# Another share of the gathers into the second stage's own tile, and fewer planned gather steps in the third

## Chip, core and metric

One core of one Trainium2 chip runs the whole layer as one program. The metric is device time in microseconds (us), the median of the runs shown. Times inside the program are read from the trace of one profiled execution and count from the start of its span.

## What is computed

One decoder layer on 256 tokens of width 2048: a mixer of two head groups, then PEER, a product-key retrieval over 128 x 128 single-neuron experts. Nearly all that follows is PEER:

```
s_half = einsum('thpd,hpkd->thpk', q, sub_keys);  v_half, i_half = top_k(s_half, 16)
top_s, pick = top_k(cand_s, 16)               # 8 heads x 16 = 128 experts per token
gates = softmax(top_s)
a    = einsum('cd,ced->ce', hc, w_u[ec])      # each token against its 128 rows of u
coef = gates * gelu(a)
out  = einsum('ce,ced->cd', coef, w_v[ec])    # weighted sum of its 128 rows of v
```

then a gated residual add and a last RMSNorm. u and v are 16384 x 2048 each.

## The kernel before

Most tokens go the dense way: every row of u and v is streamed and multiplied on TensorE (PE), and the gates are put in as a one-hot matrix. The last 64 tokens (and, for the first half of the experts, a few more) go the sparse way: for one expert slot per step, an indirect DMA gathers 128 rows of u or v (1 MB) into a tile of 128 x 2048, here called a room, and VectorE (DVE) takes one pass over it.

PEER runs in four stages of 64 blocks. In the text they are **u0, v0, u1, v1**: the u products of the first half of the experts, the v products of that half, and the same for the second half.

- A **u block** (u_block, L815 as the recording helper's line) loads 1 MB of u and makes 32 matmul passes of 128 x 144 (psU). Between blocks PE makes the gate matrix of a group of 8 tokens (pg) from one-hot tiles o and eq that DVE builds. ACT applies the gelu (tile ge), DVE multiplies it in (X).
- A **v block** (v_group, matmuls at L1088) loads 1 MB of v into a tile named raw, splits it on ACT (whi, L1062) and DVE (wlo, L1065), and makes 20 matmuls of 128 x 512 into eight accumulators (acc). wlo has two buffers, so DVE can be at most two blocks ahead of PE. At the end of v0 the eight accumulators are copied into the tile s2 (COPY s<-acc), half by ACT and half by DVE. At the end of v1 they are folded (pc, with the sparse sum sp) into the output.

**The sparse steps.** `steps_` walks a fixed plan: 32 steps m, 6 u, 16 o, 58 u, 64 v. A u, m or o step is one SCALAR_TENSOR_TENSOR on DVE with an accumulated dot product (L939); a v step adds a weighted row tile to sp (L945, first one L943). `sparse` does a step where the tables STEPS and a counter say so; `fetch` issues gathers ahead, at most `most[0]` of them. The last o step is followed by a gelu of its dot products on ACT (o_gelu, shown as ACTIVATE doto), which is put in program order among ACT's casts.

**The rooms.** `gather` takes a room: `flip` counts modulo `turns[0]`. Where it is not zero and one of the two halves of `spare[0]` is free, that half is taken; otherwise `other[0]()` gives a tile. In v0 the spare is s2 and the other one is more_room, whose tag `more` has two buffers; until the o steps are over, one of these holds h2m, the vector that they multiply with. From block 48 of v0 on, three rooms without s2 are used (rows3 is the third).

**What sets the order.** A scheduler that simulates the program chooses the order of the instructions of each engine; the order is then fixed, and on the chip each engine takes its instructions in turn. Gathers (on POOL), the sparse steps (on DVE) and what is marked with `pin` keep the order of the program among themselves, and the rest is put between them. Gathers and the DMAs that accumulate are issued by POOL (queue q0), the streams of u and v by SP (queue q1). One of POOL's is at block 20 of u1 in the code: `s<-s` adds the second half of a 64-token part of s2 onto the first by an accumulating DMA, and `s<-x2d` later refills what it read.

Of the kernel before, what the change touches and what calls it, by code (L numbers as in the profile page):

```python
# [32 lines left out]
HALF = 64  # L33
# [8 lines left out]
NS = S - TD  # L42

STEPS = dict(u0=[j for j in range(6, HALF - 6) if j % 8 != 1], v0=[j for j in range(HALF - 2) if j % 6 != 5],
             u1=[j for j in range(HALF - 6) if j % 6 != 1])


NM = 32
# [73 lines left out]
def body(ctx, tc, a, out, dbg=None, stop=None):  # L122
# [53 lines left out]
    x2 = xT.rearrange("p k s -> p (k s)").rearrange("p (t d) -> p t d", t=2)  # L176
# [38 lines left out]
    def row_load(dst, row, n=1):  # L215

        nc.gpsimd.dma_start(dst, bass.AP(tensor=row.tensor, offset=row.offset, ap=[[P // 16 * D, n], [0, P // n], [1, D]]))
# [531 lines left out]
    with ExitStack() as gctx:  # L749
# [73 lines left out]
        spare, free, other = [None], [0, 1], [None, None]  # L823
        most = [3]
        flip, turns = [0], [3]
# [164 lines left out]
        def last_room(pool):  # L990
            turn3[0] += 1
            return more_room() if turn3[0] % 3 else pool.tile([P, D], F32, name="rows3")
# [3 lines left out]
            return late.tile([P, D], F32, name="rows", tag="more", bufs=2)  # L996

        def v_group(hf, s2, late, fin=None):
            spare[0], other[0], most[0], turns[0] = x2 if hf else s2, more_room, 3, 2
            if hf:  # L1000
                fetch()
            with tc.tile_pool(name=f"vsb{hf}", bufs=1) as vb:
# [16 lines left out]
                for j in range(HALF):  # L1019
# [1 line left out]
                    tick()  # L1021
                    fixed[0] = False
                    if hf == 1:
                        if j == 0:
                            turns[0] = 3
                        elif j == 30:
                            g2 = fin("g2")
                            row_load(g2, row5, 16)
                        elif j == 34:
                            pin(nc.vector.tensor_mul(s2[:, 0, :], s2[:, 0, :], g2))  # L1030
                            nc.gpsimd.dma_start(s2[:, 0, :], x2d[:, 0, :], accum_op=OP.add)
                        elif j == 36:
                            pin(nc.vector.tensor_mul(s2[0:NS, 1, :], s2[0:NS, 1, :], g2[0:NS, :]))
                            nc.gpsimd.dma_start(s2[NS:P, 1, :], x2d[NS:P, 1, :])
                            nc.gpsimd.dma_start(s2[0:NS, 1, :], x2d[0:NS, 1, :], accum_op=OP.add)
                        elif j == 45:
                            other[0], most[0] = None, 2
                        elif j == 47:
                            gf = fin("gf")
                            nc.gpsimd.dma_start(gf, a["gfin"])  # L1040
                    elif j == 48:
                        spare[0], other[0], most[0] = None, lambda: last_room(vb), 3
                    elif j == 57:
                        other[0], most[0] = more_room, 2
# [478 lines left out]
        s2 = late.tile([P, 2, D], F32, name="s2")  # L1523
# [3 lines left out]
        dump("idx", idx)  # L1527
        uctx.close()
        v_group(0, s2, late)
        with tc.tile_pool(name="oh1", bufs=1) as oh[0]:  # L1530
            u_half(up, 1, s2)
        fixed[0] = False
        v_group(1, s2, late, lambda n: late.tile([P, D], F32, name=n, tag="more", bufs=2))


# [20 lines left out]
```

## Time and profile before

| | us |
|---|---|
| median of 3 runs | 1887.3 (1884.8 to 1891.29) |
| the profiled execution | 1885.83 |
| its span | 1883.8 |
| PE busy | 1783.8 (95%) |
| DVE busy | 1519.9 (81%) |
| POOL busy | 396.9 (21%) |

So 2.0 us of the profiled execution lie outside the span, and it stands 1.5 us below the median. PE's busy share says little by itself, since it is an average over stages and a matmul that waits inside a busy stretch is not seen in it; the chain of waits and the timelines of single engines are read instead. In a timeline a row has its start, its length, the engine, the line, the tiles, a count, and in brackets the idle time before it and who ended that. A step of 2.29 us starts 2.21 us after the one ahead of it where nothing is waited for, because reading and writing overlap at the seam. A POOL row is the time to issue a DMA, not the time in which it moves data.

### The profile page before, as it was taken

How to read it: one execution, taken by the hardware profiler on the slowest of the kernel's cores; microseconds unless marked ns; L12 is line 12 of the kernel's file. 1: busy time of each engine (PE TensorE's matmuls, PEld its weight loads, DVE VectorE, ACT ScalarE, POOL GpSimd, SP SyncE). 2: the span in 40 equal slices, each digit the busy share in tenths (PEclk: the TensorE clock that was granted, in tenths of full speed). 3: DMA queues.
4: the chain of work that ended last, by engine and by line, in shares of the span. 5: the costliest groups of instructions: out<-in, count | busy, mean ns of one | idle time of the engine just before them, and what ended most of it. 6: DMA issues, size and time to landing. Idle time of an engine off the chain costs nothing.

```text
span 1883.8 us, 29116 instructions
## 1 busy us (share of the span) xinstructions
PE 1783.8 (95%) x11560; PEld 1567.1 (83%) x11560; DVE 1519.9 (81%) x2354; ACT 707.8 (38%) x1278; POOL 396.9 (21%) x289
## 2 busy tenths in 40 slices
PE   5899999999879999999999699999999999999997
PEld 3899888798669999999997477778889898777774
DVE  7988889899689997599867799986657737889876
ACT  3444454645344421111144255541111114454554
POOL 1000001011010022111111434433112112444520
PEclk9999899999999999999999899999999999999999
DMA  8989888889888679999989899999999998999992
GB/s 343 396 324 371 300 301 301 345 302 336 306 295 322 249 262 357 425 426 424 424 347 353 314 424 425 425 379 323 426 426 426 426 418 356 407 370 360 413 357 98
DMA packets 97434, 672.51 MB, mean 357 GB/s; under 512 B 11905, under 2 KB 12177, under 8 KB 19025
## 3 DMA queue, kind: packets, MB, share of 16 engines
q1 hardware_dynamic: 66818, 467.78, 63.8%
q0 software_dynamic: 30480, 202.88, 27.0%
q8 instruction: 91, 1.49, 0.3%
q14 instruction: 45, 0.37, 0.1%
HBM read 662.81 MB, written 5.41 MB: 355 GB/s over the span
## 4 chain that ended last, share of the span: by engine, by line
PE 69%; DMA 15%; issue 7%; DVE 5%; POOL 2%; ACT 1%; SPq 0%; POOLq 0%; ACTq 0%; DVEq 0%
PE acc L1088 25%; PE psU L815 16%; PE psN L455 9%; DMA raw<-in_u 7%; PE psA L245 5%; PE psD L356 3%; PE bkB L356 2%; DMA s<-in_urow,sm__5028 2%; DVE raw L204 2%; DMA raw<-in_adaT 1%; DMA s<-in_urow,sx 1%; PE bkC L356 1%; DVE wlo L164 1%; PE bvB L408 1%; PE pg L815 1%
## 5 line engine op out<-in xcount | busy, mean ns | idle before, releaser
L815 PE MATMUL psU<-xT,raw 128*128 128x160 f32 (+1 forms) x4096 | 550.0, 295 | 16.4 <-DMA raw<-in_u 14.3
L815 PEld LDWEIGHTS psU<-xT,raw 128*128 128x128 f32 x4096 | 535.3, 191 | 21.0 <-ACT ge L815 14.2
L1088 PE MATMUL acc<-whi,cc 128*128 128x512 f32 x1512 | 371.7, 393 | 15.7 <-ACT whi L1062 15.7
L1088 PEld LDWEIGHTS acc<-whi,cc 128*128 128x128 f32 x1512 | 284.8, 189 | 86.6 <-ACT whi L1062 16.1
L1065 DVE TENSOR_TENSOR wlo<-raw,whi 128x2048 fp32r<-128x2048 f32 x126 | 288.4, 2289 | 78.9 <-issue 46.5
L1062 ACT CAST whi<-raw 128x2048 fp32r<-128x2048 f32 x126 | 240.7, 1911 | 41.8 <-DMA raw<-in_v 41.6
L1088 PE MATMUL acc<-wlo,cc 128*128 128x512 f32 x1008 | 254.9, 392 | 1.1 <-DVE wlo L1065 0.9
L204 DVE SCALAR_TENSOR_TENSOR raw<-raw,crow 128x2048 f32<-128x2048 f32 x96 | 219.3, 2285 | 22.5 <-DMA raw<-in_adaT 22.3
L163 ACT CAST whi<-raw 128x1024 fp32r<-128x1024 f32 (+1 forms) x174 | 168.6, 1019 | 165.0 <-DMA raw<-in_winA 33.1
L164 DVE TENSOR_TENSOR wlo<-raw,whi 128x1024 fp32r<-128x1024 f32 (+1 forms) x174 | 201.1, 1182 | 27.5 <-ACT whi L163 25.1
L1088 PEld LDWEIGHTS acc<-wlo,cc 128*128 128x128 f32 x1008 | 161.9, 161 | 63.7 <-DVE wlo L1065 3.3
L455 PE MATMUL psN<-whi,act 128*128 128x512 f32 x512 | 167.1, 402 | 1.4 <-ACT act L679 0.7
L815 ACT ACTIVATE X<-psU 128x160 f32<-128x160 f32 (+18 forms) x91 | 23.7, 260 | 289.1 <-PE psU L815 289.1
L455 PEld LDWEIGHTS psN<-whi,act 128*128 128x128 f32 x512 | 96.2, 190 | 25.6 <-issue 1.7
L455 PE MATMUL psN<-wlo,act 128*128 128x512 f32 x256 | 104.0, 406 | 5.7 <-DVE wlo L164 5.7
L831 POOL DMA_INDIRECT xT<-in_v,sx x25 | 79.1, 3165 | 121.9 <-DVE sp L945 79.4
L831 POOL DMA_INDIRECT rows<-in_urow,sx x35 | 69.5, 1985 | 143.6 <-DVE rows L939 109.7
L1051 ACT CAST cc<-X 128x192 fp32r<-128x192 f32 x126 | 44.0, 353 | 145.7 <-PE acc L1088 145.4
L939 DVE SCALAR_TENSOR_TENSOR rows<-rows,h2t 128x2048 f32<-128x2048 f32 x35 | 79.7, 2287 | 19.9 <-DMA rows<-in_urow,sx 19.9
L245 PE MATMUL psA<-act,whi 128*128 128x256 f32 x480 | 88.1, 286 | 3.9 <-ACT whi L163 3.9
L815 DVE TENSOR_TENSOR X<-X,ge 128x144 f32<-128x144 f32 (+17 forms) x92 | 24.2, 269 | 76.3 <-ACT ge L815 75.9
L831 POOL DMA_INDIRECT rows<-in_v,sx x28 | 51.8, 1848 | 136.5 <-DVE X L815 61.7
(376 smaller groups left out, 2595.6 us busy)
## 6 DMA issues: line engine op xcount, KB each, us to landing
raw<-in_u SPq DMA_DIRECT2D x128, 1024.0 KB, 20.6
raw<-in_v SPq DMA_DIRECT2D x128, 1024.0 KB, 11.3
raw<-in_adaT SPq DMA_DIRECT2D x96, 1024.0 KB, 7.1
raw<-in_winN SPq DMA_DIRECT2D x16, 1024.0 KB, 7.0
raw<-in_woutN SPq DMA_DIRECT2D x16, 1024.0 KB, 6.9
raw<-in_wqT SPq DMA_DIRECT2D x16, 1024.0 KB, 5.7
raw<-in_winB SPq DMA_DIRECT2D x16, 832.0 KB, 6.4
raw<-in_winD SPq DMA_DIRECT2D x12, 1024.0 KB, 6.5
```

Of the source, the lines that this page charges most:

```text
L163: nc.scalar.copy(hi[:, sl], r[:, sl])
L164: nc.vector.tensor_sub(lo[:, sl], r[:, sl], hi[:, sl].bitcast(F32))
L204: nc.vector.scalar_tensor_tensor(r, r, 1.0, crow, op0=OP.mult, op1=OP.mult, accum_out=modc[:, j, k:k + 1])
L245: nc.tensor.matmul(p_, x[:, sl], y[:, k, :], start=k == 0 and n == 0, stop=k == KB - 1 and n == 2)
L356: nc.tensor.matmul(bank[:, b, :], x[:, w], y[:, k, :], start=k == k0 and n == 0 and first, stop=k == k1 - 1 and n == 2, skip_group_check=True)
L455: nc.tensor.matmul(ps[tt], x[:, k, ts_], y[:, w], start=k == 0 and j == 0, stop=k == KB - 1 and j == 2)
L815: i = f(*a, **k)
L831: pin(nc.gpsimd.indirect_dma_start(out=r, out_offset=None, in_=src, in_offset=bass.IndirectOffsetOnAxis(ap=o, axis=0)))
L939: pin(nc.vector.scalar_tensor_tensor(r, r, 1.0, h, op0=OP.mult, op1=OP.mult, accum_out=d[:, e:e + 1]))
L1062: inorder(nc.scalar.copy(hi, r))
L1065: nc.vector.tensor_sub(lo[:, i:i + n], r[:, i:i + n], hi[:, i:i + n].bitcast(F32))
L1088: return nc.tensor.matmul(acc[c][0:m], x, w[:, c[1] * 512:(c[1] + 1) * 512], start=jj == 0 and n == 0, stop=jj == HALF - 1 and n == 2 - c[ ...
```

## The change

Two numbers. In v_group, turns starts at 3 in place of 2, in both halves (in v1 it became 3 at block 0 before): of three gathers two are sent to the halves of s2 in v0, where it was every second one. In u1 the table STEPS names three blocks in four for a sparse step, where it was five in six.

```
-             u1=[j for j in range(HALF - 6) if j % 6 != 1])
+             u1=[j for j in range(HALF - 6) if j % 4 != 1])
...
         def v_group(hf, s2, late, fin=None):
-            spare[0], other[0], most[0], turns[0] = x2 if hf else s2, more_room, 3, 2
+            spare[0], other[0], most[0], turns[0] = x2 if hf else s2, more_room, 3, 3
...
                     if hf == 1:
-                        if j == 0:
-                            turns[0] = 3
-                        elif j == 30:
+                        if j == 30:
```

The sparse steps of the three stages stay the same in number and in kind. Counted over DVE's rows between the stages' first and last passes, v0 has 52 of them before and 43 in the change, u1 44 and 51, v1 38 and 40. Three places are shown.

DVE in v0 from the pass wlo of block 15, before. A row with rows or s_6398 and h2m is an o step; s_6398 is s2.

```order
L1065 TENSOR_TENSOR wlo<-raw,whi 128x2048
L1052 TENSOR_TENSOR cc<-X_6392,cc 128x192
L939 SCALAR_TENSOR_TENSOR rows,doto<-rows,h2m 128x2048
L1065 TENSOR_TENSOR wlo<-raw,whi 128x2048
L939 SCALAR_TENSOR_TENSOR s_6398,doto<-s_6398,h2m 128x2048
L939 SCALAR_TENSOR_TENSOR rows,doto<-rows,h2m 128x2048
L939 SCALAR_TENSOR_TENSOR s_6398,doto<-s_6398,h2m 128x2048
L939 SCALAR_TENSOR_TENSOR rows,doto<-rows,h2m 128x2048
L1052 TENSOR_TENSOR cc<-X_6392,cc 128x192
L939 SCALAR_TENSOR_TENSOR s_6398,dots<-s_6398,h2t 128x2048
```

Behind the pass of block 16 stand four o steps in a row, two of them in rooms of the tag `more`.

The same place in the change, DVE again, from the pass of block 14.

```order
L1063 TENSOR_TENSOR wlo<-raw,whi 128x2048
L1050 TENSOR_TENSOR cc<-X_6392,cc 128x192
L1063 TENSOR_TENSOR wlo<-raw,whi 128x2048
L1050 TENSOR_TENSOR cc<-X_6392,cc 128x192
L1063 TENSOR_TENSOR wlo<-raw,whi 128x2048
L939 SCALAR_TENSOR_TENSOR s_6398,doto<-s_6398,h2m 128x2048 x2
L939 SCALAR_TENSOR_TENSOR rows,doto<-rows,h2m 128x2048
L1050 TENSOR_TENSOR cc<-X_6392,cc 128x192
L1063 TENSOR_TENSOR wlo<-raw,whi 128x2048
```

Three o steps stand there, one in each of three rooms, and the last one before them is three blocks up. On ACT the gelu of doto stands behind the cast of block 16 in both.

DVE at the end of v0 and the start of u1, before: from the two o tiles of the first group on. eq, iota, idx, gat belong to the one-hot tiles.

```order
L815 TENSOR_TENSOR o_11049<-eq,gat 128x512 x2
L1065 TENSOR_TENSOR wlo<-raw,whi 128x2048
L1052 TENSOR_TENSOR cc<-X_7357,cc 128x192
L815 TENSOR_TENSOR eq<-iota_5020,idx 128x512
L1065 TENSOR_TENSOR wlo<-raw,whi 128x2048
L815 TENSOR_TENSOR o_11076<-eq,gat 128x512 x2
L939 SCALAR_TENSOR_TENSOR rows,dots<-rows,h2t 128x2048 x2
L1142 COPY s_6398<-acc_8935 128x512
```

The one-hot tiles of the first two groups are made ahead of the copies. Three more copies follow.

The same place in the change, from the last copy on.

```order
L1140 COPY s_6398<-acc_8941 128x512
L939 SCALAR_TENSOR_TENSOR rows_10530,dots<-rows_10530,h2t 128x2048
L939 SCALAR_TENSOR_TENSOR rows,dots<-rows,h2t 128x2048 x2
L939 SCALAR_TENSOR_TENSOR rows_10629,dots<-rows_10629,h2t 128x2048
L939 SCALAR_TENSOR_TENSOR rows,dots<-rows,h2t 128x2048 x2
L939 SCALAR_TENSOR_TENSOR rows_10758,dots<-rows_10758,h2t 128x2048
L815 TENSOR_TENSOR o_11040<-iota_5020,idx 128x1024
L815 TENSOR_TENSOR eq<-iota_5020,idx 128x512
L815 TENSOR_TENSOR o_11067<-iota_5020,idx 128x1024
L939 SCALAR_TENSOR_TENSOR rows,dots<-rows,h2t 128x2048
L815 TENSOR_TENSOR o_11042<-eq,gat 128x512 x2
```

Eight steps of the plan that stood among v0's blocks now stand between the copies and the second one-hot tile of the first group, o_11042. On PE three u blocks stand ahead of the first pg in both. On POOL `s<-s` now stands behind the gather of the third of these eight, and `s<-x2d` behind that of the fifth; before, they stood behind the twelfth and the fifteenth gather counted from the same one.

DVE at the end of v1, before.

```order
L945 SCALAR_TENSOR_TENSOR sp<-xT,dots,sp 128x2048
L1065 TENSOR_TENSOR pair_15282<-raw,pair_15282 128x1024 x2
L1065 TENSOR_TENSOR pair_15288<-raw,pair_15288 128x1024 x2
L945 SCALAR_TENSOR_TENSOR sp<-xT,dots,sp 128x2048
L1104 TENSOR_TENSOR tg<-pc,g_14288 128x512
```

One step (xT is the spare tile of v1, with two halves) stands behind the last passes of v.

The same in the change.

```order
L945 SCALAR_TENSOR_TENSOR sp<-xT,dots,sp 128x2048
L1063 TENSOR_TENSOR pair_15272<-raw,pair_15272 128x1024 x2
L1063 TENSOR_TENSOR pair_15278<-raw,pair_15278 128x1024 x2
L945 SCALAR_TENSOR_TENSOR sp<-xT,dots,sp 128x2048 x4
L1102 TENSOR_TENSOR tg<-pc,g_14274 128x512
```

Four steps stand there, in two rooms; before each of the last two its gather has to wait for the step two ahead of it.

## The prediction

> **What bounds the kernel now.** I read the chain of waits first, then the stages by windows, then PE's timeline where the chain leaves PE.
>
> ```profile
> 1094.92 185.14 PE acc L1088 x809
> 1281.22 12.04 PE psU L815 x96
> 1293.27 25.64 DMA raw<-in_u
> ...
> 1330.49 33.44 DMA raw<-in_u
> 1368.25 34.90 DMA raw<-in_u
> ...
> 1471.23 34.84 DMA raw<-in_u
> ...
> 1571.32 272.20 PE acc L1088 x1192
> 1849.01 4.63 DVE pair L1065 x4
> 1853.64 2.27 DVE sp L945
> ```
>
> v0 and v1 are PE: 809 matmuls in 185.14 us, so a block of 20 takes 4.577 us. u1 is partly the stream of u: four stretches of it are waits for DMA. The very end goes over DVE, its last sparse step included.
>
> ```profile
> 971.00:1281.00 310.00, 292.96 (x1269) 224.74 (x1267) 270.57 (x242) 146.04 (x188) 114.42 (x49) 0.97 0.95 384
> 1281.00:1571.00 290.00, 273.86 (x2479) 269.23 (x2480) 172.82 (x251) 45.40 (x170) 56.07 (x50) 0.99 0.99 402
> 1571.00:1884.00 313.00, 300.20 (x1299) 229.36 (x1297) 260.10 (x201) 155.36 (x212) 111.93 (x41) 0.99 0.88 341
> ```
>
> The rows are v0, u1, v1; behind PE, PEld, DVE, ACT and POOL stand the granted clock, the DMA share and GB/s. In u1 the queues are full (0.99), in v1 not (0.88). v0 has 17 us in which PE does nothing, though no engine is full. The change touches nothing ahead of v0. Four places decide; I sum them against the profiled execution, 1885.83.
>
> **A, the stall in the middle of v0: removed, -17.5.**
>
> ```profile
> 1044.94 1.09 PE L1088 MATMUL acc<-whi,cc 128*128 128x512 f32 x4
> 1061.73 3.75 PE L1088 MATMUL acc<-whi,cc 128*128 128x512 f32 x8 [15.70 <-ACT whi L1062]
> ...
> 1059.43 0.21 ACT L815 ACTIVATE doto<-doto 128x16 f32<-128x16 f32 x1 [24.69 <-DVE rows L939]
> 1059.55 0.33 ACT L1051 CAST cc<-X 128x192 fp32r<-128x192 f32 x1
> 1059.79 1.89 ACT L1062 CAST whi<-raw 128x2048 fp32r<-128x2048 f32 x1
> ...
> 1038.39 2.28 DVE L939 SCALAR_TENSOR_TENSOR s<-s,h2m 128x2048 f32<-128x2048 f32 x1
> 1046.86 2.29 DVE L939 SCALAR_TENSOR_TENSOR rows<-rows,h2m 128x2048 f32<-128x2048 f32 x1 [6.18 <-DMA rows<-in_urow,smo]
> ...
> 1057.09 2.29 DVE L939 SCALAR_TENSOR_TENSOR rows<-rows,h2m 128x2048 f32<-128x2048 f32 x1 [5.52 <-DMA rows<-in_urow,smo]
> ```
>
> Of the tag `more` only one room is free until the o steps are done, and every second gather wants it. So the last four o steps take two rounds of gather and step (waits of 6.18 and 5.52); ACT holds the gelu for 24.69 us, and the casts of the next block, queued behind it, starve PE for 15.70. The row of 3.75 us for 8 matmuls shows a slow start too: 8/20 of 4.577 is 1.83. From 1061.73 to 1094.92, which is 1.83 into the seventh block, are 33.2 us where 6 x 4.577 + 1.83 = 29.3 would do: 3.9 more. Lost in all: 19.6.
>
> With two gathers in three to s2, three rooms carry the round, so the three o steps behind block 16 have had their gathers issued three blocks (13.7 us) or more ahead. They then end at 1038.39 + 3 x 2.21 = 1045.0, the gelu, the cast of cc and the cast of whi at 1045.0 + 0.21 + 0.33 + 1.89 = 1047.4, where PE runs dry at 1046.0; DVE's wlo behind it costs another half. That leaves about 2 us of stall: -17.5. Bounds: -19.5 if nothing is left, -13 if one late gather holds the three. The rest of v0 has 3 steps in 5 blocks (5 x 2.5 + 3 x 2.3 = 19.4 of 22.9 us on DVE) and stays PE's.
>
> **B, the spilled steps at the start of u1: +27.** The nine steps that v0 no longer has must be paid in u1, and eight of them, with `s<-s` and `s<-x2d` among their gathers on POOL, stand ahead of o_11042 on DVE, for which PE waits at its first pg.
>
> ```profile
> 1281.22 12.03 PE L815 MATMUL psU<-xT,raw 128*128 128x144 f32 x96 [0.48 <-ACT s L1142]
> 1293.08 0.63 PE L815 MATMUL pg<-o,o 128*128 128x64 f16 x16
> ...
> 1310.46 0.63 PE L815 MATMUL pg<-o,o 128*128 128x64 f16 x16
> ...
> 1319.05 6.94 PE L815 MATMUL psU<-xT,raw 128*128 128x144 f32 x32 [3.51 <-DMA raw<-in_u]
> ...
> 1279.03 2.75 POOL L831 DMA_INDIRECT rows<-in_urow,sx  x1 [9.70 <-DVE rows L939]
> ...
> 1284.27 0.99 POOL L1476 DMA_DIRECT2D s<-s  x1
> 1288.81 1.03 POOL L831 DMA_INDIRECT rows<-in_urow,sx  x1 [3.56 <-DVE rows L939]
> ...
> 1300.12 0.56 POOL L1034 DMA_DIRECT2D s<-x2d  x1 [5.97 <-DMA s<-s]
> ...
> 1280.88 2.49 DVE L1142 COPY s<-acc 128x512 f32<-128x512 f32 x4
> 1286.24 2.29 DVE L939 SCALAR_TENSOR_TENSOR rows<-rows,h2t 128x2048 f32<-128x2048 f32 x1 [2.88 <-DMA rows<-in_urow,sx]
> ...
> 1304.80 2.29 DVE L939 SCALAR_TENSOR_TENSOR rows<-rows,h2t 128x2048 f32<-128x2048 f32 x1 [6.51 <-DMA rows<-in_urow,sx]
> ```
>
> The first of these gathers lands 1286.2 - 1279.0 = 7.2 us after its issue; the one issued behind `s<-s` needs 1304.8 - 1288.8 = 16.0, and `s<-s` itself 1300.1 - 1284.3 = 15.8, for which POOL waits at `s<-x2d`. Before, nothing on PE hung on either.
>
> Now the new order, in us from the end of v0's matmuls (1280.7 before), with 7.7 from a room's release to the next use (7.2 and half a us of issue). The three steps and the copies end at 1.4; step 1 runs to 3.7, step 2 to 6.0; step 3 (room released at -1.1) starts at 6.6, to 8.9; step 4 (room of step 1) 11.4 to 13.7; step 5 13.7 to 16.0. `s<-s` goes out at 1.4 and lands at 17; behind it POOL issues gather 6 at 17.9, which lands at 25.3: step 6 to 27.6, step 7 to 29.9; o_11040 and what goes with it 1.6, step 8 2.3, o_11042 0.7: 34.5. PE comes to its first pg at 13.5 (three blocks of 4.0 behind the copies), so it stands 21 us. After a stand the next block is slow (6.94 against 4.1: 2.8 more), and the third pg, behind two more steps whose rooms come free late, waits some 2.4 again. PE reaches its fourth pg at 57.0; before, at 1310.46 - 1280.7 = 29.7. That is +27. Low bound: `s<-s` alone in the queue lands at 11.5, all gathers in 7.4, and the same sum gives +22. High: every gather behind `s<-s` needs the 16 us and they queue up; gather 6 lands at 34, 7 at 39, 8 at 44, and the sum is +40. I take +27, since PE's stand stops the stream of u, so the queue is emptier than at 1288.8.
>
> On the slow block the Trainium skill ("TensorE: Matmul & The Clock Gate", Part 1: The HAM clock gate) says that PE falls to half its clock after an idle window of about 3.4 us and needs as much busy time to come back. The trace agrees: 3.51 us of waiting were followed by the one block of 6.94 us. By it a stand of any length costs the same 2 to 3 us, as I have it.
>
> **C, the rest of u1: -15.5.**
>
> ```profile
> PE psU L815 <- DMA raw<-in_u: 14.3, 20, 3.5
> ```
>
> ```profile
> 1519.52 47.29 PE L815 MATMUL psU<-xT,raw 128*128 128x144 f32 x384
> ```
>
> ```profile
> GB/s 343 396 324 371 300 301 301 345 302 336 306 295 322 249 262 357 425 426 424 424 347 353 314 424 425 425 379 323 426 426 426 426 418 356 407 370 360 413 357 98
> ```
>
> The first row is what PE waited for u in u1, 20 times; with the slow block 17.1. In the change three steps in four blocks ask for 7 MB where PE needs 4 x 3.94 for blocks (47.29 us for twelve at the end) and about 0.9 for pg; at 426 GB/s, the most that a slice of the page shows, 7 MB take 17.2 against 16.7. And the stand of B lets SP fill its eight tiles, 20 us of stream, ahead of time. So nearly all of these waits go. Bounds -17 (all) and -10 (the steps come in clumps of one per block, as where the waits are now). Note that the stage does not get fewer gathers by the new table: with the spill it has 51 steps, not 44.
>
> **D, the end of v1: +14.**
>
> ```profile
> 1853.55 2.35 DVE L945 SCALAR_TENSOR_TENSOR sp<-xT,dots,sp 128x2048 f32<-128x2048 f32 x1
> ...
> 1855.95 1.13 PE L1130 MATMUL pc<-sp,sel 128*128 128x512 f32 x2 [0.48 <-DVE sp L945]
> ...
> 1836.10 2.74 POOL L831 DMA_INDIRECT xT<-in_v,sx  x1 [1.99 <-DVE sp L945]
> ...
> DMA to landing us min/median/max: 8.8/8.8/8.8
> ```
>
> PE waits for sp already (0.48): nothing covers the end of the steps. Four steps now stand where one stood, in two rooms, and the last gather, with the streams over, still took 8.8 us. Step one runs to 1855.9. Step two's room is released at 1849.0 by the step ahead of the pair passes; with 8.3 (between 7.7 and 9.05, which is 8.8 and the 0.25 before issue) it starts at 1857.3, to 1859.6. Step three 1855.9 + 8.3 = 1864.2, to 1866.5; step four 1859.6 + 8.3 = 1867.9, to 1870.2: 14.4 later than now, and the fold and output behind it move by as much: +14 (11 with 6.9, 16 with 9.05 and a slow PE). The remaining blocks of v1 carry the same load as now.
>
> **The sum:** -17.5 + 27 - 15.5 + 14 = +8, so 1893.8 for a profiled execution, and with the 1.5 between that and the median, 1895.3: **1895**, slower by 0.4%.
>
> **Rivals.**
>
> 1. *The spill meets a crowded queue.* B at its high bound: -17.5 + 40 - 15.5 + 14 = +21, 1908. For it: gathers took 16 us and more just there (16.0 above). Against: PE's stand quiets SP.
> 2. *Light gathers, no change.* B +22 and D +11 give -0.5 with C -16: 1887. For it: 7.2 us at 1279. Against: the accumulating transfer stands among them.
> 3. *Faster: the spilled steps run nearly back to back.* The place is B, the price what DVE itself needs. The quickest gather in the trace landed in 5.3 us:
>
> ```profile
> DMA to landing us min/median/max: 5.3/5.3/5.3
> ```
>
>    With that, and `s<-s` no slower, step 6 ends at 15.9 and o_11042 at 23.5; PE stands 10, B is +14, D +10: -17.5 + 14 - 16 + 10 = -9.5, 1878. It decides from a B below 13 on. Against: of the gathers at v0's end none was under 7. Beside it, the Trainium skill ("DMA: Bandwidth & Descriptors", Anatomy of one DMA — SWDGE (gpsimd) path) fits a DMA from GpSimd by 2.0 us and the bytes at 436 GB/s, an estimate of 4.4 for 1 MB, by which this rival would be the likeliest; the trace's 7.2 to 8.8 on near-idle queues speak against it.
> 4. *A isn't removed*, because a gather of the last round is late and ACT holds the casts as long as now: -2 + 27 - 15.5 + 14 = +23.5, 1911.
>
> **Chances.** Forecast 0.46 (its own range 1889 to 1901), rivals 0.17, 0.22, 0.11, 0.04. About 0.3%, 5.7 us, is what a measurement of this kernel can tell from no change: 1881.6 to 1893.0. Slower: 0.35 of the forecast, rivals 1 and 4, 0.02 of rival 2: 0.58. Same: 0.11, 0.18 of rival 2, 0.01 of rival 3: 0.30. Faster: 0.12. The range, 1883 to 1909, takes in rivals 1 and 2 and leaves out most of 3 and 4.
>
> **What would show it.** A: no idle of PE over 3 us at L1088 in v0, and v0's matmuls end near 1263. B: on PE an idle of 15 to 25 us ahead of the first pg, ended by DVE; on POOL a wait at `s<-x2d` for `s<-s` of about 14. C: PE's waits for raw<-in_u below 6 in u1. D: PE's wait at the first pc<-sp near 14. The forecast is wrong where the stand at the first pg is under 10 or where DVE is late at one of the v blocks, since I took their cover from the rows of before.

## The result

The changed kernel took 1907.7 us in the median of 7 runs (1898.15 to 1910.66). Against the kernel before, run beside it, the ratio is 1.0108, 95% interval 1.0081 to 1.0135: about 20 us slower. One of the seven runs of the kernel before took 4588 us and is an outlier; the other six lie between 1881.6 and 1891.3. The prediction said 1895, 1883 to 1909. Sign and range hold, the size was 2.5 times too small, and the time is that of rival 1. That the range holds is partly luck: B and C both came out beyond their own bounds, in opposite directions (below).

The profiled execution after took 1902.72 with a span of 1900.9, 17.1 above the span before. Its start was an early one: v0 began at 964.17 where before it began at 968.08, and nothing of the change lies ahead of that. Without these 3.9 the profile shows 21.0, close to the 20.4 between the medians.

Three windows, at the times that were v0, u1 and v1 before (u1 now starts at 1260.26, so the first window takes in some 20 us of it):

```profile
971.00:1281.00 310.00, 298.38 (x1348) 232.75 (x1346) 257.62 (x227) 145.01 (x190) 105.77 (x47) 0.99 0.97 373
1281.00:1571.00 290.00, 260.11 (x2394) 259.07 (x2395) 178.12 (x268) 46.14 (x170) 47.97 (x50) 0.94 0.97 400
1571.00:1884.00 313.00, 295.00 (x1262) 223.74 (x1261) 257.04 (x176) 148.00 (x194) 99.15 (x41) 0.97 0.88 339
```

Behind the length stand PE, PEld, DVE, ACT and POOL, the granted clock, the DMA share and GB/s. PE does nothing for 11.6 us of the first window, and 10.1 of them belong to the start of u1: v0 no longer has its 17 us without PE. What is new is the clock of 0.94 in the second window: PE stood there long enough to lose it (the windows of 0.50 under B).

**Where the time went.** I cut the span at five places of PE's timeline: the first matmul of v0, the first psU of u1, the fourth pg of u1, the end of the last psU, the first pc<-sp. The piece up to the fourth pg is called the head of u1, the one behind it the rest.

| | v0 | head of u1 | rest of u1 | v1 | tail |
|---|---|---|---|---|---|
| before | 313.1 | 29.2 | 260.9 | 284.6 | 27.8 |
| after | 296.1 | 72.2 | 236.5 | 301.1 | 30.7 |
| difference | -17.0 | +43.0 | -24.4 | +16.5 | +2.9 |
| predicted | A -17.5 | B +27 | C -15.5 | D +14 | (in D) |

**A.** PE in v0, at the place of the 15.70 before:

```profile
1041.04 1.09 PE L1086 MATMUL acc<-whi,cc 128*128 128x512 f32 x4
1043.44 2.13 PE L1086 MATMUL acc<-whi,cc 128*128 128x512 f32 x8 [1.30 <-ACT whi L1060]
1045.76 2.12 PE L1086 MATMUL acc<-wlo,cc 128*128 128x512 f32 x8 [0.20 <-DVE wlo L1063]
```

The stall is 1.30 and 0.20, and the blocks behind it run at full speed (20 matmuls from 1047.72 to 1052.26, 4.54 us).

**B.** PE at the start of u1:

```profile
1260.26 12.03 PE L815 MATMUL psU<-xT,raw 128*128 128x144 f32 x96 [1.40 <-DVE s L1140]
1305.71 0.21 PE L815 MATMUL pg<-o,o 128*128 128x64 f16 x1 [33.42 <-DVE o L815]
1306.87 5.48 PE L815 MATMUL psU<-xT,raw 128*128 128x144 f32 x32
...
1321.82 1.01 PE L815 MATMUL pg<-o,o 128*128 128x64 f16 x16 [5.00 <-ACT X L815]
...
1332.51 0.63 PE L815 MATMUL pg<-o,o 128*128 128x64 f16 x16
```

DVE's spilled steps there, and POOL's issues:

```profile
1260.13 2.28 DVE L939 SCALAR_TENSOR_TENSOR rows<-rows,h2t 128x2048 f32<-128x2048 f32 x1
1262.34 2.28 DVE L939 SCALAR_TENSOR_TENSOR rows<-rows,h2t 128x2048 f32<-128x2048 f32 x1
1269.71 2.29 DVE L939 SCALAR_TENSOR_TENSOR rows<-rows,h2t 128x2048 f32<-128x2048 f32 x1 [5.09 <-DMA rows<-in_urow,sx]
1278.11 2.29 DVE L939 SCALAR_TENSOR_TENSOR rows<-rows,h2t 128x2048 f32<-128x2048 f32 x1 [6.10 <-DMA rows<-in_urow,sx]
1285.63 2.29 DVE L939 SCALAR_TENSOR_TENSOR rows<-rows,h2t 128x2048 f32<-128x2048 f32 x1 [5.22 <-DMA rows<-in_urow,sx]
1294.29 2.29 DVE L939 SCALAR_TENSOR_TENSOR rows<-rows,h2t 128x2048 f32<-128x2048 f32 x1 [6.35 <-DMA rows<-in_urow,sx]
1299.14 2.29 DVE L939 SCALAR_TENSOR_TENSOR rows<-rows,h2t 128x2048 f32<-128x2048 f32 x1 [2.56 <-DMA rows<-in_urow,sx]
...
1258.08 0.94 POOL L831 DMA_INDIRECT rows<-in_urow,sx  x1 [13.62 <-DVE rows L939]
1259.59 0.96 POOL L1474 DMA_DIRECT2D s<-s  x1 [0.57 <-issue]
1262.69 2.85 POOL L831 DMA_INDIRECT rows<-in_urow,sx  x1 [2.14 <-DVE rows L939]
1265.84 0.96 POOL L831 DMA_INDIRECT rows<-in_urow,sx  x1 [0.30 <-issue]
1273.44 0.56 POOL L1032 DMA_DIRECT2D s<-x2d  x1 [6.64 <-DMA s<-s]
1274.31 0.97 POOL L831 DMA_INDIRECT rows<-in_urow,sx  x1 [0.30 <-issue]
```

The gathers issued at 1258.08, 1262.69, 1265.84 and 1274.31 belong to the steps at 1269.71, 1278.11, 1285.63 and 1294.29: 11.6, 15.4, 19.8 and 20.0 us. What the queues did in these windows:

```profile
1264.00:1270.00 6.00, 6.00 (x51) 6.00 (x50) 0.91 (x3) 0.58 (x2) 2.50 (x2) 1.00 1.02 213
...
1276.00:1282.00 6.00, 0.00 (x0) 0.00 (x0) 2.30 (x2) 0.00 (x0) 0.94 (x1) 0.50 1.06 388
1282.00:1288.00 6.00, 0.00 (x0) 0.00 (x0) 2.30 (x2) 0.00 (x0) 0.00 (x0) 0.50 0.99 257
1288.00:1294.00 6.00, 0.00 (x0) 0.00 (x0) 0.00 (x0) 0.00 (x0) 0.94 (x1) 0.50 1.00 415
```

From 1276 on PE does nothing, its clock falls to 0.50, and the queues stay full (1.06, 0.99, 1.00) up to 1294. They empty only at the end of the stand, when the stream of u moves nothing any more and all bytes are of POOL's queue:

```profile
1300.00:1306.00 6.00, 0.21 (x1) 0.20 (x2) 5.96 (x10) 0.00 (x0) 0.41 (x1) 0.50 0.25 107
```

**C.** In the rest of u1 PE waited for u not once. Two blocks and a pg, before and then after:

```profile
1364.06 4.16 PE L815 MATMUL psU<-xT,raw 128*128 128x144 f32 x32 [0.71 <-DMA raw<-in_u]
1368.06 0.63 PE L815 MATMUL pg<-o,o 128*128 128x64 f16 x16
1368.97 4.16 PE L815 MATMUL psU<-xT,raw 128*128 128x144 f32 x32 [0.28 <-DMA raw<-in_u]
```

```profile
1341.36 8.09 PE L815 MATMUL psU<-xT,raw 128*128 128x144 f32 x64
1349.29 0.63 PE L815 MATMUL pg<-o,o 128*128 128x64 f16 x16
1349.75 12.01 PE L815 MATMUL psU<-xT,raw 128*128 128x144 f32 x96
```

After, they take 1349.75 - 1341.36 = 8.39. Before, the next block began at 1373.86, so they took 9.80, 1.41 more, though the brackets up to there (0.28 and the 0.72 of the next block) list 1.00: each of the two waits cost 0.2 more than is listed.

**D.** DVE, POOL and PE at the end of v1:

```profile
1856.59 2.93 POOL L831 DMA_INDIRECT xT<-in_v,sx  x1 [5.12 <-DVE sp L945]
1859.83 0.94 POOL L831 DMA_INDIRECT xT<-in_v,sx  x1 [0.30 <-issue]
1864.20 2.35 DVE L945 SCALAR_TENSOR_TENSOR sp<-xT,dots,sp 128x2048 f32<-128x2048 f32 x1 [5.49 <-DMA xT<-in_v,sx]
1867.76 2.35 DVE L945 SCALAR_TENSOR_TENSOR sp<-xT,dots,sp 128x2048 f32<-128x2048 f32 x1 [1.21 <-DMA xT<-in_v,sx]
...
1870.16 2.07 PE L1128 MATMUL pc<-sp,sel 128*128 128x512 f32 x2 [14.25 <-DVE sp L945]
```

### The profile page after: what moved, and what is told of

Read it like the earlier page. It is cut to its first block, busy times and chain, and to the rows that moved or that the text cites. A ratio compares the mean times of both kernels' runs of the same rounds, so it can differ in the third digit from the quotient of the medians.

```text
span 1900.9 us, 29122 instructions
## 1 busy us (share of the span) xinstructions
PE 1779.0 (94%) x11560; PEld 1565.7 (82%) x11560; DVE 1520.2 (80%) x2354; ACT 707.8 (37%) x1278; POOL 369.5 (19%) x289
## 4 chain that ended last, share of the span: by engine, by line
PE 77%; DMA 8%; issue 6%; DVE 6%; POOL 2%; ACT 1%; SPq 0%; POOLq 0%; ACTq 0%; DVEq 0%
PE acc L1086 29%; PE psU L815 21%; PE psN L455 8%; PE psA L245 5%; PE psD L356 3%; PE bkB L356 2%; DMA raw<-in_adaT 2%; DMA s<-in_urow,sm__5028 2%; DVE raw L204 2%; DVE wlo L164 1%; PE pg L815 1%; PE bkC L356 1%; PE bvB L408 1%; DMA rows<-in_urow,sx 1%; DMA raw<-in_urow,sm__5028 1%
## 5 line engine op out<-in xcount | busy, mean ns | idle before, releaser
L1086 PEld LDWEIGHTS acc<-whi,cc 128*128 128x128 f32 x1512 | 283.9, 188 | 72.2 <-issue 1.9
L204 DVE SCALAR_TENSOR_TENSOR raw<-raw,crow 128x2048 f32<-128x2048 f32 x96 | 219.1, 2282 | 20.4 <-DMA raw<-in_adaT 20.0
L831 POOL DMA_INDIRECT xT<-in_v,sx x28 | 73.8, 2636 | 178.3 <-DVE sp L945 79.2
L939 DVE SCALAR_TENSOR_TENSOR rows<-rows,h2t 128x2048 f32<-128x2048 f32 x30 | 68.6, 2289 | 31.2 <-DMA rows<-in_urow,sx 31.2
L831 POOL DMA_INDIRECT s<-in_urow,sx x23 | 57.1, 2480 | 152.8 <-DVE cc L1050 90.2
L245 PEld LDWEIGHTS psA<-act,whi 128*128 128x128 f32 x480 | 74.7, 192 | 3.8 <-ACT whi L163 3.8
```

Of the source, the lines that this page charges most:

```text
L204: nc.vector.scalar_tensor_tensor(r, r, 1.0, crow, op0=OP.mult, op1=OP.mult, accum_out=modc[:, j, k:k + 1])
L245: nc.tensor.matmul(p_, x[:, sl], y[:, k, :], start=k == 0 and n == 0, stop=k == KB - 1 and n == 2)
L831: pin(nc.gpsimd.indirect_dma_start(out=r, out_offset=None, in_=src, in_offset=bass.IndirectOffsetOnAxis(ap=o, axis=0)))
L939: pin(nc.vector.scalar_tensor_tensor(r, r, 1.0, h, op0=OP.mult, op1=OP.mult, accum_out=d[:, e:e + 1]))
L1086: return nc.tensor.matmul(acc[c][0:m], x, w[:, c[1] * 512:(c[1] + 1) * 512], start=jj == 0 and n == 0, stop=jj == HALF - 1 and n == 2 - c[ ...
```

## Experiments

Two theories at first. *Mine, from the two traces:* the loss is the spill (B) and the four last steps (D), and each belongs to one of the two numbers of the change. *The rival:* the thin table of u1 is what makes it slow. Later, for the size of B, *the accumulating transfer* against *the stream of u*. In the last theory below, u1 as a whole takes what its queues have to carry, and head and rest only share it out; the runs support it in part.

All kernels, cut at the same five places (the start of v0 differs from run to run by some us and stands for itself):

| | start | v0 | head | rest | u1 | v1 | tail | median | ratio to before (95%) |
|---|---|---|---|---|---|---|---|---|---|
| before | 968.1 | 313.1 | 29.2 | 260.9 | 290.1 | 284.6 | 27.8 | 1887.3 | |
| after | 964.2 | 296.1 | 72.2 | 236.5 | 308.8 | 301.1 | 30.7 | 1907.7 | 1.0108 (1.0081 to 1.0135) |
| only_turns | 967.3 | 296.1 | 68.5 | 241.3 | 309.9 | 288.1 | 27.9 | 1893.2 | 1.0038 (1.0022 to 1.0054) |
| only_u1 | 967.2 | 314.2 | 29.2 | 251.8 | 281.0 | 299.2 | 30.4 | 1893.8 | 1.0043 (1.0025 to 1.0060) |
| turns_back_u6 | 970.5 | 295.8 | 38.9 | 248.0 | 286.9 | 289.0 | 27.8 | 1871.3 | 0.9920 (0.9898 to 0.9941) |
| turns_back_u4 | 966.1 | 295.8 | 39.5 | 241.5 | 280.9 | 293.5 | 30.2 | 1869.2 | 0.9911 (0.9886 to 0.9936) |
| after_late | 968.9 | 296.1 | 62.5 | 244.1 | 306.6 | 302.6 | 29.5 | 1905.8 | 1.0110 (1.0092 to 1.0129) |
| ring5 | 967.3 | 296.1 | 66.3 | 239.4 | 305.7 | 300.9 | 30.8 | 1904.0 | 1.0103 (1.0068 to 1.0138) |
| late_ring5 | 966.5 | 296.1 | 59.6 | 247.2 | 306.8 | 303.1 | 29.5 | 1906.0 | 1.0122 (1.0085 to 1.0160) |
| no_ss | 972.8 | 296.1 | 62.7 | 236.5 | 299.2 | 305.1 | 30.4 | 1898.0 | 1.0066 (1.0047 to 1.0085) |
| after_end46 | 966.0 | 296.1 | 69.3 | 236.5 | 305.8 | 293.8 | 29.4 | 1894.1 | 1.0049 (1.0026 to 1.0072) |
| best | 966.6 | 295.7 | 39.2 | 249.4 | 288.6 | 282.2 | 27.7 | 1863.8 | 0.9890 (0.9869 to 0.9911) |
| best_late | 967.3 | 297.8 | 37.4 | 256.3 | 293.6 | 283.3 | 27.7 | 1871.5 | 0.9926 (0.9900 to 0.9952) |
| best_30 | 967.8 | 296.2 | 53.0 | 243.9 | 296.9 | 284.9 | 27.7 | 1875.3 | 0.9950 (0.9933 to 0.9968) |

Each ratio is against runs of the kernel before that were taken with it, and their medians lie between 1883.5 and 1887.3; so ratios are compared here, not medians. The stages are those of one execution each. How far such a stage differs without any edit shows in the head: up to the first pg DVE has the same order in after, only_turns and after_end46, and their heads are 72.2, 68.5 and 69.3.

**Each number alone.** only_turns is the change without the new table:

```
-             u1=[j for j in range(HALF - 6) if j % 4 != 1])
+             u1=[j for j in range(HALF - 6) if j % 6 != 1])
```

> Only the first number of the change: turns is 3 in v0, the table of u1 is as before (five blocks in six). The planned order has the same eight spilled steps ahead of the first group of u1 and one step behind the last passes of v1, as before. If the loss is the spill (A -22, B +44, as read from the two traces), it stays: v0's matmuls end near 1259, PE stands 30 to 35 us ahead of its first pg; of the waits for u (C, -25 in the change) a part comes back since the gathers are five in six again, and D is gone: together slower than before by 5 to 25 us, 1892 to 1912. The rival, that the thinner table of u1 makes the change slow, expects 1865 here.

only_u1 is the kernel before with it:

```
-             u1=[j for j in range(HALF - 6) if j % 6 != 1])
+             u1=[j for j in range(HALF - 6) if j % 4 != 1])
```

> Only the second number: u1 has three steps in four blocks, turns as before. The planned order has no spill at the start of u1 and four steps behind the last passes of v1. By the terms of the two traces: the stall in v0 (15.7 on PE) stays, B is gone, C -15 to -25, D +20: 1882 to 1892. If the gain in u1 needed the stand of B, during which SP fills its tiles, C is under -10 and the time is 1895 or more.

The first pg of u1 in only_turns; then PE's waits over v0 to v1 in only_u1 (total, times, longest):

```profile
1305.07 0.21 PE L815 MATMUL pg<-o,o 128*128 128x64 f16 x1 [29.65 <-DVE o L815]
```

```profile
PE acc L1088 <- ACT whi L1062: 17.4, 1, 17.4
PE pc L1130 <- DVE sp L945: 14.0, 1, 14.0
PE psU L815 <- DMA raw<-in_u: 11.1, 14, 3.5
```

A and B belong to turns: v0 is 296.1 with it and 314.2 without, PE's stand at the first pg 29.65 with it and none without. D belongs to the table: 14.6 in v1 and 2.6 in the tail with it, 3.5 and 0.1 without. So each number alone loses some 0.4%, and for different reasons; the rival falls as the only cause, since only_turns keeps the old table and is slower too. only_turns came out within its range; only_u1 2 us above it, mostly because C alone is worth 9.1 (rest 251.8) and not 15 to 25. C is where the two overlap: the stand alone, with the old table, brought 19.6 of it, the thin table alone 9.1, both 24.4. So most of C came with B. It does not take a stand at the first pg, though: turns_back_u4 below has none, and with PE held for 8.2 at the third pg its rest is 241.5, 19.4 under that before.

**The room rule while it is needed.** turns is 3 up to block 14 of v0 only:

```
+                    if hf == 0 and j == 14:
+                        turns[0] = 2
```

with the table of u1 as before (turns_back_u6) and thin (turns_back_u4).

> Turns is 3 in v0 up to block 14 and 2 from there on, so the o steps have their three rooms and the rest of v0 has the old ones; the table of u1 is as before. Planned: no more than two spilled steps, which stand among the first one-hot tiles, and one step at v1's end. By the terms: A -22, B 0 to +8, C and D none: 1865 to 1873. The rival is that u1 is bound by its DMA whatever v0 gains, so that what PE gains in v0 comes back as waits for raw<-in_u: 1880 to 1887.

> As the one before, with the thin table of u1 (three in four). Planned: two spilled steps, three steps behind the last passes of v1. By the terms: A -22, B 0 to +8, C -15 to -25, D +8 to +16: 1850 to 1870. If C needed the stand, 1875 or more.

v0 is 295.8 in both, so all of A comes from the rooms of the o steps; the third that goes on behind them only makes the planned order put steps off into u1 (43 of them stand in v0 with it, 50 here). Without the spill no pg waits for its one-hot tiles; the third one waits for ACT:

```profile
PE pg L815 <- ACT X L815: 7.6, 1, 7.6
```

(turns_back_u6.) Both are faster than before, by 0.8 and 0.9%. That u1 would hand back what v0 gained did not happen: u1 is 286.9 and 280.9, under the 290.1 before. turns_back_u4 has C (u1 -9.2) and part of D (v1 and tail +11.3, PE's wait for sp 8.9).

**What made B 43 and not 27.** Three kernels on the change, in which DVE's order of the eight spilled steps and the first one-hot tiles is untouched. after_late holds s<-s back on POOL:

```
-                if hf and j == 20:
-                    nc.gpsimd.dma_start(s2[0:NS, 1, :], s2[NS:P, 1, :], accum_op=OP.add)
+                if hf and j == 28:
+                    pin(nc.gpsimd.dma_start(s2[0:NS, 1, :], s2[NS:P, 1, :], accum_op=OP.add))
```

> The change, with the accumulating transfer s<-s (and s<-x2d behind it) held back on POOL to block 28 of u1. DVE's and PE's planned orders at the start of u1 are the same. In the change the stretch from v0's last matmul to the fourth pg took 73.6 (30.2 before) and PE stood 33.4 at the first pg. If s<-s at the head of POOL's queue is what made the spilled steps slow, the stand falls to 12 or less (as with gathers of 7 us), the stretch to 50 or less, the time by 20. If it is the stream of u, of which SP issues eight tiles ahead while PE stands, the stand falls by no more than the 6.6 that POOL waited for s<-s and the 1.5 MB that the two transfers move: 25 to 30, the stretch 64 to 70, the time by 3 to 9.

ring5 gives the stream of u five tiles instead of eight for the first blocks:

```
-                if hf and j == 4:
+                if hf and j == 24:
                     set_ring(late, raw=5, whi=3)
```

> The change, with five tiles for the stream of u in place of eight up to block 24 of u1: while PE stands, SP can issue 3 MB less ahead. s<-s stays where it is. If the stream crowds the gathers, PE's stand at the first pg falls from 33.4 by about the 7 us that 3 MB take at 426 GB/s, to 24 to 29. If s<-s alone is at fault, it stays at 32 to 35. Behind the stand the rest of u1 (236.3 in the change, 260.6 before) should get longer by up to 10 in both cases, since fewer tiles have been filled: that is the part of C that the stand paid for.

late_ring5 has both edits.

> Both of these together. If s<-s and the stream share the blame, the stand falls to 15 to 24, by about the sum of the two falls. If the gathers are slow of themselves (7 to 8 us from a room's release to the next use with nothing else in the queues), the stand does not go under 15, since six rounds in three rooms are still two rounds of gather and step behind each other.

The first pg in after_late, in ring5, in late_ring5, and for comparison in after_end46 (below), which edits nothing ahead of it:

```profile
1301.74 0.21 PE L815 MATMUL pg<-o,o 128*128 128x64 f16 x1 [24.69 <-DVE o L815]
```

```profile
1303.14 0.21 PE L815 MATMUL pg<-o,o 128*128 128x64 f16 x1 [27.75 <-DVE o L815]
```

```profile
1294.42 0.21 PE L815 MATMUL pg<-o,o 128*128 128x64 f16 x1 [19.76 <-DVE o L815]
```

```profile
1304.46 0.21 PE L815 MATMUL pg<-o,o 128*128 128x64 f16 x1 [30.41 <-DVE o L815]
```

From 33.42 the stand falls by 8.7, 5.7 and 13.7. Without an edit there it is 29.65 in only_turns and 30.41 in after_end46, so the falls of after_late and late_ring5 are clear, and that of ring5 alone is hardly more than the difference between executions. The smaller ring gives 4.9 more on top of after_late. Neither cause carries the stand alone: the gathers shared full queues with s<-s, and, as far as these runs show, with the stream of u, which SP issues ahead while PE stands. The time that s<-s takes does not set the stand by itself: in only_turns it landed some 9.4 us after its issue, where it took 13.9 in the change, and PE stood 29.65. The stream had its part by a route that I had put the other way round in the prediction (below).

But none of the three is faster than the change by its ratio: 1.0110, 1.0103 and 1.0122 against 1.0108. I had expected 3 to 9 us from after_late. Their heads are 9.7, 5.9 and 12.6 shorter and their rests 7.6, 2.9 and 10.7 longer, so u1 is 306.6, 305.7 and 306.8 against 308.8 (and 305.8 in after_end46). What the stand loses comes back for the most part as waits for u: 6.1, 1.8 and 9.1 us in the three rests. In the change the rest was at its floor: 236.5, with no wait for u, and the same 236.5 in after_end46 and no_ss.

**What u1 has to carry.** no_ss leaves s<-s and the s<-x2d behind it out:

```
-                if hf and j == 20:
-                    nc.gpsimd.dma_start(s2[0:NS, 1, :], s2[NS:P, 1, :], accum_op=OP.add)
...
-                            nc.gpsimd.dma_start(s2[NS:P, 1, :], x2d[NS:P, 1, :])
```

> The change without s<-s and without the s<-x2d that refills what it read (left out: 64 tokens of the last stage lack the first half's products and their residual). Two transfers of 0.5 MB leave u1's queues; the planned order of DVE is the same. While they were in flight the change moved 213 and 257 GB/s at a full DMA share in two stretches of 6 us, where 426 is the most: so they cost the queues about 3 and 2.4 us more than others, and by that 5 to 6 in all, their own bytes counted at 426 GB/s included. If u1's length is set by what its queues have to carry, u1 (309.9 to 310.1 in the change) is 5 to 8 shorter and the time 1897 to 1903. If only waits that are handed round count, as with s<-s held back, u1 stays within 2 of 308 to 310 and the time at 1904 to 1908. In both cases PE's stand at the first pg falls to 22 to 27.

```profile
1305.25 0.21 PE L815 MATMUL pg<-o,o 128*128 128x64 f16 x1 [24.27 <-DVE o L815]
```

The stand is that of after_late (24.69). But here the rest stays at 236.5 where it was 244.1 with the transfer held back, and u1 is 299.2: 9.6 shorter. The ratio fell from 1.0108 to 1.0066, about 8 us. Put off, the transfers gave nothing that can be told; taken out, they gave more in u1 than the 5 to 8 expected. So on the change u1 behaves as if it took what its queues have to carry, and the place of PE's stand in it decided little. A plainer reading fits no_ss as well: the gathers of the head are no longer delayed by the transfers, and nothing is put into the rest, which stays at its floor. The steps of before and after fit: u1 has 44 of them before and 51 after, and is 18.7 longer, 2.7 per step, where 1 MB takes 2.5 at 426 GB/s. It is no law of the stage, though. only_turns has 54 steps in u1, three more than the change, and is 1.1 longer; turns_back_u6 has 47, three more than before, and is 3.2 shorter; turns_back_u4 and best have 44, as before, and are at 280.9 and 288.6; only_u1 has 42 and is at 281.0. How the steps are spread weighs several us, and that part I did not settle.

**The end of v1 alone.** after_end46 spreads v1's steps to end by block 46:

```
-                        sparse(left[0] / max(1, 56 - j) if j not in (34, 36) else 0)
+                        sparse(left[0] / max(1, 46 - j) if j not in (34, 36) else 0)
```

> The change, with the steps of v1 spread so that they end by block 46 in place of 56. The planned order of v0 and u1 is the same; behind the last passes of v1 stand two steps in place of four, one in each room, so that no gather waits for a step behind the passes. If D is two rounds of gather and step at the end, PE's wait at the first pc<-sp falls from 14.25 to 1 to 5, the end moves up by 10 to 17 and the time is 1891 to 1898. If D came from v1 having more steps in all (40 against 38), it stays at 10 or more and the time over 1900.

```profile
1861.66 1.90 PE L1128 MATMUL pc<-sp,sel 128*128 128x512 f32 x2 [2.87 <-DVE sp L945]
```

With two steps behind the last passes, one in each room, the wait is 2.87 in place of 14.25, and the ratio 1.0049 in place of 1.0108, some 11 us. In the traces 8.6 of that lie in v1 and the tail; the head of u1, which the edit leaves alone, is 2.9 shorter as well. v1 has its 40 steps in both. D was the second round of gather and step in two rooms, as the prediction had it. In return DVE is late by 3.7 at one block of v1.

**Together.** best takes turns back at block 14, has four gathers in five in u1 and the end of v1 by block 46:

```
+             u1=[j for j in range(HALF - 6) if j % 5 != 1])
...
+                    if hf == 0 and j == 14:
+                        turns[0] = 2
...
+                        sparse(left[0] / max(1, 46 - j) if j not in (34, 36) else 0)
```

> Turns 3 in v0 up to block 14 and 2 from there on, four gathers in five in u1, and in v1 the steps are spread so that they end by block 46 in place of 56; planned, two steps among the first one-hot tiles of u1 and none behind the last passes of v1. The first part gave 1871 with the old table of u1; D is nothing here (0 to -2 against before, as the one step behind the passes goes too), C -15 to -20, A -15 to -20, B +10: 1858 to 1866. The rival is that steps crowded into the first 46 blocks of v1 make DVE late there: waits for wlo of 5 or more in v1, 1870 or more.

It is the fastest: 1863.8, ratio 0.9890 (0.9869 to 0.9911), within its range. Its span is 23.0 under that before: v0 -17.4, u1 -1.5, v1 and tail -2.5, and 1.5 of the start. DVE is not late in v1.

best_late is best with s<-s held back as in after_late.

> The kernel called best, with s<-s held back to block 28 of u1. Held back in the changed kernel, it took 8.7 us off the stand and gave nothing to the time, since the rest of u1 got longer by as much. If u1's length is set by what its queues have to carry, the same is seen here: the stretch up to the fourth pg (40.3) shorter by 3 to 8, the rest of u1 longer by as much, the time 1861 to 1866 against 1864. If the wait of the third pg (7 us here) is lost for good, the time falls to 1855 to 1859.

Neither expectation held: 1871.5, by the ratios some 7 slower than best, u1 +5.0. Another 2.1 lie in v0, where the edit changes nothing. The head is 1.8 shorter, but the rest 6.9 longer; one wait for u is now long enough to cost PE its clock (0.50 granted from 1417 to 1419):

```profile
1414.78 9.76 PE L815 MATMUL psU<-xT,raw 128*128 128x144 f32 x64 [2.11 <-DMA raw<-in_u]
```

Two blocks take 8.09 otherwise. That the held-back transfer meets the stream where no tile is ahead would explain it; it was not tried apart.

best_30 is best with turns taken back at block 30.

> As the kernel called best, but turns goes back to 2 at block 30 of v0 and not at 14. Planned: v0 has 48 steps in place of 50, u1 46 in place of 44, three steps stand ahead of the first one-hot tile of u1. If each step that spills into u1 costs what its 1 MB takes there (2.5 us at 426 GB/s), 4 to 8 slower than best: 1866 to 1873. If the steps in u1 are free as long as PE doesn't stand at the first pg, the same as best, 1861 to 1866.

1875.3, 11 slower than best with two more steps in u1, more than either theory gave. The bytes would be 5; the head is 13.8 longer, and PE's wait there stands out:

```profile
PE pg L815 <- ACT X L815: 13.9, 1, 13.9
PE pg L815 <- DVE o L815: 4.7, 2, 2.9
```

ACT's X waits for a product on DVE, and that stands behind seven steps (five in best). The first two pg wait for their one-hot tiles too, 4.7 together. So the third spilled step costs more than its bytes here, by waits in the head. A version of turns_back_u4 without steps behind v1's passes (u1 280.9 and best's v1) was not run.

## Why the prediction came out as it did

**A was right.** -17.5 was forecast and v0 is 17.0 shorter, as in all kernels that have three rooms for the o steps (295.7 to 296.2; 297.8 in best_late). The 1.30 and 0.20 that remain are the "about 2 us of stall".

**B was mis-sized, +43 in place of +27, and beyond my high bound of +40.** The step that failed is the gathers' price: "7.7 from a room's release to the next use" for steps 3 to 5, and the choice of +27 "since PE's stand stops the stream of u, so the queue is emptier than at 1288.8". The order of the steps and the length of s<-s (13.9 from 1259.59 to 1273.44, against the 15.6 used) were right. That POOL waits at s<-x2d was right too, but for 6.64, where I had named about 14 as a sign. Counted from the end of v0's last matmul (1258.86), step 3 began at 10.85 where I had 6.6, step 4 at 19.25 (11.4), step 5 at 26.77 (13.7), step 6 at 35.43 (25.3). So the gathers took 11.6 to 20.0 and not 7.2, and PE stood 33.4 and not 21. What I took from the row at 1279.0, 7.2 us, was measured in these windows of the kernel before:

```profile
1276.00:1282.00 6.00, 5.52 (x27) 4.14 (x26) 6.00 (x8) 2.25 (x4) 2.75 (x1) 1.00 0.67 265
1282.00:1288.00 6.00, 6.00 (x51) 6.00 (x51) 3.12 (x4) 0.00 (x0) 2.87 (x3) 1.00 0.90 339
```

The queues had room there, at shares of 0.67 and 0.90, but near-idle, as I called them under rival 3, they were not; in the change the share was 1.0. The prediction used one fact in two directions: in C, PE's stand "lets SP fill its eight tiles"; in B, the same stand was to empty the queue. While SP fills tiles, it is the queue's load. ring5 and late_ring5 put that part at some 5 us of the stand (5.7 and 4.9, with the spread above); s<-s and its refill have the larger one (8.7 in after_late). How the remaining excess over 7.2 divides is not shown.

That is the mechanism of rival 1. For it I had quoted the 16.0 of the gather behind s<-s, against it only the quiet that wasn't there. That its time, 1908, is the measured one is luck, however: its terms were off by 0.5 (A), 3.0 (B), -8.9 (C) and 5.4 (D), which cancel.

By the Trainium skill ("DMA: Bandwidth & Descriptors", Queues, rings and completion order) an engine goes round-robin between the queues that have work; by that, q0 gets about half of 426 GB/s while SP's queue is full, and three gathers and s<-s with its refill, 4.2 MB, take an estimated 20 us; the gathers issued from 1265.84 to 1280.68 took 18.5 to 20.0, so the trace agrees. It also shows the halves: POOL's queue and SP's moved 1.16 and 1.16 MB from 1276 to 1282, 1.31 and 1.18 from 1288 to 1294, and 0.75 and 0.79 from 1282 to 1288, where the total was 257 GB/s and not 426. The fit from the same page that the prediction set beside rival 3, 4.4 us for 1 MB, is far from them.

**C was mis-sized, -24.4 in place of -15.5, beyond its bound of -17.** I took the listed idle (14.3) as the waits' cost. A block that waits is 4.16 long and not 3.94 in a row of blocks, and so the two waits above cost 0.2 more each than is listed. Twenty waits then cost an estimated 14.3 + 4.1 = 18.4, and with 2.8 for the slow block and the 1.5 that PE waited for ACT's ge, 22.7; the other 1.7 I can't place. That the waits go altogether I put down to the tiles that are filled while PE is held up in the head: only_u1, where it is not, gets 9.1.

**B and C hang together**, which the sum did not have: together +18.6 where I had +11.5. The experiments show that, in the changed kernel, most of what is cut from B is given back in C as long as the same is to be carried. One term for u1, seven more steps (51 against 44) at 2.5 us, gives +17.5, and the numbers for it stood in the prediction, in the part on C. But that is hindsight: by the same term turns_back_u6 would have a longer u1 than before, and it has a shorter one.

**D's mechanism and its wait were right**: 14.25 against a forecast of 14.4 later, from a last gather that took 7.9 (1859.83 to 1867.76). Two things were left out. PE comes back from that wait at half clock (0.50 granted up to 1876; the first pc<-sp takes 2.07 where before it took 1.13), and the tail is 2.9 longer. And DVE is late at one block of v1, a condition under which the prediction said it would be wrong:

```profile
1764.83 2.10 PE L1086 MATMUL acc<-wlo,cc 128*128 128x512 f32 x8 [2.12 <-DVE wlo L1063]
```

That makes +19.4 in all. On the clock, the Trainium skill's rule ("TensorE: Matmul & The Clock Gate", Part 1: The HAM clock gate) held as far as B shows it: after a stand of 33.42 the next block took 5.48, no more extra than the block behind 3.51 before. Behind D's wait of 14.25 the clock stayed at 0.50 for some six us after PE came back (1870.16 to 1876), behind B's stand for some four.

**The sum:** -17.0 + 43.0 - 24.4 + 19.4 = +21.0, against +8.

## What to carry to other kernels

Where a stage's queues are full, count what it has to carry before you price single waits: on the changed kernel a stand that was shortened came back as waits for the stream, unless transfers were taken out. The count is a first check only: kernels here with the same 44 steps in u1 differ by 9 us there. An engine that stands does not empty the queues as long as a prefetching stream has tiles to fill: here the share stayed near 1.0 up to 1294 and fell to 0.25 only when the stream moved nothing. And a rule that helps at one place (three rooms for sixteen steps) should end there: kept on, with the old table, it made u1 309.9 where it is 286.9 when ended at block 14.

## What the runs showed of the hardware

The accumulating transfer from on-chip memory to on-chip memory was dearer than its bytes. s<-s, 0.5 MB on 64 partitions, took between 8.1 us (best) and 15.6 us (before). In a part of its flight and of the refill's the queues moved 213 and 257 GB/s at a full share (1264 to 1270 and 1282 to 1288 under B; in the 12 us between them, 406 and 388). With s<-s held back, they moved 426 while PE stood:

```profile
1282.00:1288.00 6.00, 0.00 (x0) 0.00 (x0) 3.03 (x4) 0.00 (x0) 1.00 (x2) 0.50 1.01 426
```

(after_late.) Without the two transfers u1 was 9.6 us shorter, where their 1 MB would take 2.5 at 426 GB/s. Why they cost more than their bytes no run shows.
